# A scan's output tiles from a pool of four, and a convolution's kernels by one transfer

## The chip, the cores and the metric

The kernel runs on one core of one Trainium2 chip. The metric is the device time of one execution in microseconds (us), taken over several runs; a profile of one execution stands beside it. The engines are named as in the profile: PE is TensorE's matmul and PEld its weight load, DVE is VectorE, ACT is ScalarE, POOL is GpSimd, SP is SyncE, whose queue issues most transfers.

## The reference

One layer of a hybrid network runs over two sequences with the same weights: 256 context tokens and 2048 latent tokens of 1024 channels. What matters here, cut down:

```
h = rms_norm(x, g_pre) * (1 + scale) + shift
z, xbc, dt_raw, ga, gb, gsil = split(h @ w_in)
# group (i): a scan in chunks of 128 tokens, in both directions
xs, b_in, c_in = split(silu(depthwise_conv(xbc, width 5)))
y = scan_forward + scan_backward + d_skip * xs        # 16 heads of 64 channels
y_ssd = rms_norm(y * silu(z), norm_g)
# group (ii): gated depthwise convolution of width 31
hc = depthwise_conv(ga * sigmoid(gb), conf_conv_w) + conf_conv_b
y_conf = silu(layer_norm(hc)) * silu(gsil)
out = x + gate * rms_norm(concat(y_ssd, y_conf) @ w_out, g_post)
```

For the context the convolution of group (ii) runs along the 256 tokens. For the latent tokens, a grid of 32 rows by 64 columns, it runs down the rows, each column for itself. Besides the two outputs the final scan states of the context are returned.

## The kernel before

The 18 chunks of 128 tokens (two of context, sixteen of latent) are worked in two halves of ten and eight. In each half the input projection is computed channel block by channel block (128 channels), as three matmuls of split float32 operands for every 128 rows of the weights (mm_cm, L428 to L436). load_w (L384) fetches the weights. In the second half it reads the split weights that the first half has stored (wh and wl from whd and wld, L390 and L391, 512 KB each), into a pool of three buffers each.

The order of the projection blocks is: the xbc blocks, with their short convolution and a store to XB (L535); eight gate units for the conformer group (gab_unit, tiles gb and ga, whose result gl is stored at L598 into GL); eight units for z and eight for gsil (silu_unit, tile sp, stored at L611). All of these are generators. The work of the scan and of the convolutions is laid in between them step by step (interleave, merge), and a scheduler with a simulated timeline then decides the final order on each engine outside the parts that are kept in program order by hand.

pass_a (L702) is the forward scan of one chunk, in two groups g of eight heads. It loads xT and bc (L705, L707), and decay rows lb through ScalarE's queue (load_lb, L718; four buffers for each direction). GpSimd masks them (L730), ScalarE takes the exponentials (el at L727, the decays at L738), VectorE mixes the two directions (L742, L743). TensorE transposes x (px, L750), makes the diagonal part py (L774), the state's part po (L781) and the new states pst (L787 to L789). The output tile of a group, yg, lives through three VectorE steps and a store: skip (L808) takes a tile from a pool of two and writes d_skip * x into it (L810); close (L813) adds py (L815) and the state's part (L817), and the store at L818 sends it to YP on SP's queue. skip of a later group therefore waits until the store of the tile two groups before has landed.

The latent convolution takes one block of 128 channels at a time, j = 0 to 7 (lat_conv, L673). It is a set of small matmuls: the kernels of a block come as a table kd (128 partitions of 32 by 32 values), are turned by ScalarE into kt (L679), and 256 matmuls of 32 by 32 by 64 (cp, L690) multiply kt with x, the gated input read back from GL. VectorE empties the banks into cvv (L694), and four stores a block go to CV (L699). lat_load (L663) fetches kd and x in four quarters of 32 partitions, kd from the padded kernel array wconv (L670), x from GL (L671); both have two buffers, so block j + 1 is fetched while block j is worked on. PSUM tiles of the scan and of this convolution share a ring of five banks ("ss").

In the second half the pool lp (L1015) holds kd, x (tile cx), kt, cvv, the biases cbb and the context convolution's buffers cg; it is opened when the pools of the short convolution are closed. The scan's other tiles are in pool pa, which is open over both halves. The eight blocks of the latent convolution and the last four of the context convolution (ctx_conv, L640) are laid between the projection units of the second half, together with the scan of chunks 9 to 17 (L1020 to L1029). Behind them the backward scan and the output projection follow, in an order written by hand from L1335 on.

Of the kernel before, what the change touches and what calls it, by code (L numbers as in the profile page):

```python
# [8 lines left out]
F32 = mybir.dt.float32  # L9
# [8 lines left out]
P = 128  # L18
# [66 lines left out]
def backbone_kernel(ctx, tc, xa, xt_in, cols, rows, wconv, conf_b, gp_row, bg_row, state0, w_mod, w_dt, w_in, w_out,  # L85
# [3 lines left out]
    V, S, T, DMA = (InOrder(tc, e) for e in (nc.vector, nc.scalar, nc.tensor, nc.sync))  # L89
# [30 lines left out]
    def place(i):  # L120

        return (0, i) if i < HT[0] else (1, i - HT[0])
# [66 lines left out]
    pa = ph_a.enter_context(tc.tile_pool(name="pa", bufs=1))  # L189
# [473 lines left out]
    def lat_load(j, lp):  # L663
        kd = lp.tile([P, 32, 32], F32, tag="kd", name=f"kd{j}", bufs=2)
        x = lp.tile([P, 32, 64], F32, tag="cx", name=f"cx{j}", bufs=2)
        lat_in[j] = kd, x
        for a in range(4):
            rs = slice(a * 32, (a + 1) * 32)
            src = bass.AP(tensor=wconv.tensor, offset=(j * 4 + a) * 64 * 32, ap=[[32, 32], [1, 1024]])
            DMA.dma_start(kd[rs].rearrange("p r g -> p (r g)"), src)  # L670
            DMA.dma_start(x[rs], GL[j][:, 256:].rearrange("(g a) (r w) -> a r g w", a=4, w=64)[a])  # L671

    def lat_conv(j, lp, cbb, more):  # L673
        if j not in lat_in:
            lat_load(j, lp)
        kd, x = lat_in.pop(j)
        yield
        kt = lp.tile([P, 32, 32], F32, tag="kt", name=f"kt{j}", bufs=1)
        S.copy(kt[:, :, ::-1].rearrange("p g r -> p r g"), kd)  # L679
        if more(j + 1):  # L680
            lat_load(j + 1, lp)
        yield
        vt = lp.tile([P, 32, 64], F32, tag="cvv", name=f"cvv{j}", bufs=1)
        for h in range(2):
            ps = {a: bank("ss", f"cp{j}_{a}") for a in (2 * h, 2 * h + 1)}
            for q in range(8):
                for u in range(4):
                    for a in ps:
                        rs = slice(a * 32, (a + 1) * 32)
                        T.matmul(ps[a][u * 32:(u + 1) * 32, q * 64:(q + 1) * 64], kt[rs, u * 8 + q, :], x[rs, u * 8 + q, :],  # L690
                                 start=True, stop=True)
            yield
            for a in ps:
                V.scalar_tensor_tensor(vt[:, a::4, :], ps[a].rearrange("p (c w) -> p c w", w=64), 0.5,  # L694
                                       cbb[:, j, a::4].unsqueeze(2).to_broadcast([P, 8, 64]), MUL, ADD)
            yield
        for u in range(4):
            c0 = j * P + u * 32
            DMA.dma_start(CV[c0:c0 + 32, 256:].rearrange("c (r w) -> r c w", w=64), vt[u * 32:(u + 1) * 32])  # L699


    def pass_a(i):  # L702
        half, il = place(i)
# [102 lines left out]
        yg = {}  # L806

        def skip(g):  # L808
            yg[g] = pa.tile([P, 4, P], F32, tag="yg", name=f"yg{i}{g}", bufs=2)
            V.tensor_tensor(yg[g], xT[:, 4 * g:4 * g + 4, :],  # L810
                            cv[:, C_D + 4 * g:C_D + 4 * g + 4].unsqueeze(2).to_broadcast([P, 4, P]), MUL)

# [35 lines left out]
        decay(0, 1)  # L848
        mask(1, 0)
        skip(0)  # L850
        load_lb(1, 1)
        yield
        weigh(0, 1)
        mix(0, 1)
        decay(1, 0)
        mask(1, 1)
        skip(1)
        yield
        diag(0, 0)
# [155 lines left out]
    lp = ph_l.enter_context(tc.tile_pool(name="lp", bufs=1, side="right"))  # L1015
# [122 lines left out]
    def norms(i, yz, nq):  # L1138

        pm = bank("ss", f"pm{i}")  # L1140
        src = [(c, e, t[1]) for c, e, t in ((0, 4.0 * EPS, yz), (1, EPS, nq)) if t]
        for c, e, t in src:
            T.matmul(pm[:, c:c + 1], t, ones[:, 0:1], start=True, stop=True)
        rs = []
        for c, e, t in src:
            ms = p1.tile([P, 1], F32, tag=f"ms{c}", name=f"yms{i}{c}", bufs=2)
            V.tensor_scalar(ms, pm[:, c:c + 1], 1.0 / D, e, MUL, ADD)
            rs.append((c, rstd_of(p1, ms, f"yr{i}{c}")))
        return rs
# [31 lines left out]
    def conf_load(i):  # L1181
        n = p2.tile([P, 8, P], F32, tag="cn", name=f"cn{i}", bufs=2)
        DMA.dma_start(n, CV[:, i * P:(i + 1) * P].rearrange("(c p) t -> p c t", p=P))
        return n
# [20 lines left out]
    def gs_load(i):  # L1205
        gs = p2.tile([P, 8, P], F32, tag="gs", name=f"gsl{i}", bufs=1)
        DMA.dma_start(gs, chan_slice(GS, i))
        return gs
# [57 lines left out]
    i = order[0]  # L1266
# [21 lines left out]
    for b in range(2):  # L1288
        for m, u in enumerate(last):
            run(take(u, 8))  # L1290
            if b == 0 and m == 1:
                rs = norms(i, yz, None)
# [18 lines left out]
            if b == 1 and m == 0:  # L1311
                rs = norms(i, None, nq)
                nq = conf_sqsum(i1, vv[1][0])
            if b == 1 and m == 1:
                n, v = nn[0], vv[0][0]
# [3 lines left out]
            if b == 1 and m == 2:  # L1319
                gs0, v0, n = gs_load(i), v, nn[1]  # L1320
# [17 lines left out]
    i, nxt, nx2 = order[:3]  # L1338
    banks(i)
    out_part(pso[i], yh, 0, 1)  # L1340
    rs = norms(nxt, yz, nq)
# [42 lines left out]
    n, n2 = n2, conf_load(order[3])  # L1384
    yh = yhn

    for a, i in enumerate(order[1:], 1):
# [7 lines left out]
        rs = None if last else norms(nxt, yz, nq)  # L1395
# [46 lines left out]
        if a + 3 < NT:  # L1442
            ssd_load(order[a + 3])
            n, n2 = n2, conf_load(order[a + 3])
        else:
            n = n2
# [72 lines left out]
```

## Time and profile before

| | |
|---|---|
| time, median of 3 runs | 1862.05 us (1860.89 to 1865.44) |
| the profiled execution's own time | 1862.69 us |
| its span, first to last instruction | 1860.9 us |
| mean granted TensorE clock | 0.983 |
| PE busy | 1797.5 us |
| DVE, ACT, POOL busy | 1212.7, 867.4, 167.5 us |
| transfers on SP's queues and ACT's queue, all together | 375.22 MB, mean 202 GB/s |

The stretches: until about 270 us the first half's xbc blocks, from 270 to 730 us the first half's scan, until 917 us the second half's xbc blocks, from 917 to about 1330 us the second half's scan with the latent convolution, then the backward scan and the output projection. Times in the answers of the trace are counted from the span's start. A row of the timeline gives start, duration, engine, line, operation, tiles and shape, and in brackets the engine's idle time before it with what ended it; "SPq" and "ACTq" rows are the issue of transfers on these queues, and their duration is that of the issue, not of the transfer. In the chain that ended last, a DMA row is the time from issue to landing. The granted clock of a stretch is a share of TensorE's full speed.

### The profile page before, as it was taken

The numbers are of one execution on the slowest core, as the hardware profiler recorded it, in microseconds if no ns is written. First come the engines' busy times: TensorE is split into PE (matmuls) and PEld (weight loads), VectorE is DVE, ScalarE is ACT, GpSimd is POOL, SyncE is SP. The second block draws the span as 40 slices with busy tenths as digits, with TensorE's granted clock in tenths as the row PEclk, the third lists the DMA queues.
The fourth block names the chain that finished last, engine by engine and source line by source line (L and its number), as shares of the span: only waits on it lengthen the run. The fifth ranks groups of instructions, "written<-read, shape, count | busy, mean of one in ns | idle before, by whom it ended". The sixth has DMA issues, their size and how long they took to land.

```text
span 1860.9 us, 29891 instructions
## 1 busy us (share of the span) xinstructions
PE 1797.5 (97%) x11167; PEld 1482.9 (80%) x11167; DVE 1212.7 (65%) x1846; ACT 867.4 (47%) x1958; POOL 167.5 (9%) x281
## 2 busy tenths in 40 slices
PE   5899999999999999999999889899999999999998
PEld 3688887888888888888877667677887888888886
DVE  4488867565666762587457475868347887777763
ACT  4646424444465441834235445553245545454441
POOL 0002001111111000100001011110000111111110
PEclk9899999999999999999999899899999999999999
DMA  9556565574776664446598799685877666566632
GB/s 319 201 202 224 198 222 196 168 237 153 239 271 232 202 214 162 163 152 210 175 223 239 163 255 227 220 226 193 278 237 247 184 184 170 173 171 170 187 102 79
DMA packets 304253, 375.22 MB, mean 202 GB/s; under 512 B 84198, under 2 KB 203622, under 8 KB 304108
## 3 DMA queue, kind: packets, MB, share of 16 engines
q1 hardware_dynamic: 283372, 335.56, 58.1%
q10 hardware_dynamic: 20736, 37.76, 7.1%
q8 instruction: 88, 1.44, 0.3%
q14 instruction: 57, 0.47, 0.1%
HBM read 243.66 MB, written 129.59 MB: 201 GB/s over the span
## 4 chain that ended last, share of the span: by engine, by line
PE 84%; DMA 8%; ACT 2%; DVE 2%; issue 1%; SPq 1%; POOL 0%; ACTq 0%; POOLq 0%; DVEq 0%
PE op L81 20%; PE sp L433 7%; PE sp L434 7%; PE sp L435 7%; PE xp L434 5%; PE xp L435 5%; PE xp L433 5%; PE ga L433 3%; PE ga L435 2%; PE ga L434 2%; DMA lb<-lt 2%; PE gb L433 2%; PE gb L435 2%; PE gb L434 2%; PE py L774 2%; PE po L781 2%
## 5 line engine op out<-in xcount | busy, mean ns | idle before, releaser
L738 ACT ACTIVATE lb<-lb,WB 128x128 f32<-128x128 f32 x576 | 184.4, 391 | 173.5 <-POOL lb L730 159.6
L433 PE MATMUL sp<-hh,wh 128*128 128x512 f32 (+1 forms) x640 | 239.9, 375 | 0.0
L435 PE MATMUL sp<-hh,wl 128*128 128x512 f32 (+1 forms) x640 | 237.3, 371 | 0.0
L434 PE MATMUL sp<-hl,wh 128*128 128x512 f32 (+1 forms) x640 | 237.3, 371 | 0.0
L433 PE MATMUL xp<-hh,wh 128*128 128x512 f32 (+1 forms) x464 | 171.4, 371 | 2.0 <-ACT hh L329 2.0
L434 PE MATMUL xp<-hl,wh 128*128 128x512 f32 (+1 forms) x464 | 171.7, 370 | 0.0
L435 PE MATMUL xp<-hh,wl 128*128 128x512 f32 (+1 forms) x464 | 171.5, 370 | 0.0
L730 POOL TENSOR_SCALAR_AFFINE_SELECT lb<-lb 128x512 f32<-128x512 f32 x144 | 105.2, 733 | 730.4 <-ACT el L727 392.1
L530 DVE SCALAR_TENSOR_TENSOR cva<-raw,cwh,cva 128x1280 f32<-128x1280 f32 (+1 forms) x96 | 142.0, 1487 | 19.6 <-ACT cva L524 17.6
L435 PEld LDWEIGHTS sp<-hh,wl 128*128 128x128 f32 x640 | 121.4, 190 | 21.1
L433 PEld LDWEIGHTS sp<-hh,wh 128*128 128x128 f32 x640 | 121.7, 190 | 20.6
L434 PEld LDWEIGHTS sp<-hl,wh 128*128 128x128 f32 x640 | 121.6, 190 | 20.0
L433 PE MATMUL ga<-hh,wh 128*128 128x512 f32 (+1 forms) x320 | 121.1, 378 | 5.0 <-DMA wh<-whd 4.7
L75 DVE SCALAR_TENSOR_TENSOR cg<-cg,cv 128x256 f32<-128x256 f32 x240 | 121.2, 505 | 3.3
L433 PE MATMUL gb<-hh,wh 128*128 128x512 f32 (+1 forms) x320 | 120.4, 376 | 0.6 <-DVE gth L597 0.6
L435 PE MATMUL ga<-hh,wl 128*128 128x512 f32 (+1 forms) x320 | 119.1, 372 | 0.0
L434 PE MATMUL ga<-hl,wh 128*128 128x512 f32 (+1 forms) x320 | 118.8, 371 | 0.0
L435 PE MATMUL gb<-hh,wl 128*128 128x512 f32 (+1 forms) x320 | 118.5, 370 | 0.0
L434 PE MATMUL gb<-hl,wh 128*128 128x512 f32 (+1 forms) x320 | 118.4, 370 | 0.0
L742 DVE TENSOR_TENSOR lb<-lb,lb 128x512 f32<-128x512 f32 x72 | 50.5, 702 | 92.0 <-ACT lb L738 70.6
L433 PEld LDWEIGHTS xp<-hh,wh 128*128 128x128 f32 x464 | 88.1, 190 | 16.9 <-ACT hh L329 2.3
L434 PEld LDWEIGHTS xp<-hl,wh 128*128 128x128 f32 x464 | 87.9, 189 | 14.3
(269 smaller groups left out, 3758.6 us busy)
## 6 DMA issues: line engine op xcount, KB each, us to landing
lb<-lt ACTq DMA_DIRECT2D x144, 256.0 KB, 4.4
wr<-in_w_in SPq DMA_DIRECT2D x88, 256.0 KB, 5.4
whd<-wh SPq DMA_DIRECT2D x44, 512.0 KB, 4.0
wld<-wl SPq DMA_DIRECT2D x44, 512.0 KB, 5.2
wh<-whd SPq DMA_DIRECT2D x44, 512.0 KB, 4.3
wl<-wld SPq DMA_DIRECT2D x44, 512.0 KB, 5.9
xT<-xb SPq DMA_DIRECT2D x18, 512.0 KB, 4.1
yp<-yg SPq DMA_DIRECT2D x36, 256.0 KB, 4.6
```

The lines of the kernel that those rows point to most:

```text
L75: return self._tc.keep_in_program_order(getattr(self._eng, name)(*a, **k))
L81: return lambda *a, **k: self._tc.keep_in_program_order(f(*a, **k))
L433: T.matmul(ps[:, :BN], wh[:, k, :], hh[:, k, :], start=(k == 0), stop=False)
L434: T.matmul(ps[:, :BN], wh[:, k, :], hl[:, k, :], start=False, stop=False)
L435: T.matmul(ps[:, :BN], wl[:, k, :], hh[:, k, :], start=False, stop=(k == KT - 1))
L530: V.scalar_tensor_tensor(a[:, :n], raw[:, t:t + n], cwh[:, ct * 5 + t:ct * 5 + t + 1], a[:, :n], MUL, ADD)
L730: G.affine_select(E[g, hq, d], E[g, hq, d], pattern=[[0, 4], [sg, P]], compare_op=ALU.is_ge, fill=NEG, base=0, channel_multiplier=-sg)
L738: S.activation(lb[:, h, :], lb[:, h, :], AF.Exp, bias=WB[:, i, c + h:c + h + 1])
L742: V.tensor_tensor(a, a, E[g, hq, 1], ADD)
L774: T.matmul(py[g][j * HD:(j + 1) * HD, q * P:(q + 1) * P], xt[g][:, h * HD:(h + 1) * HD], E[g, hq, 0][:, t, :], start=True, stop=True)
L781: T.matmul(po[g][:, q * P:(q + 1) * P], Sf[g][:, q * P:(q + 1) * P], bc[:, 2 + g, :], start=True, stop=True)
```

## The change

Two places are edited. In lat_load the four transfers of kd, one for each quarter of 32 partitions, become one transfer of 512 KB, placed ahead of the four transfers of x. Its source is written as four blocks (2048 values apart) of 32 rows (32 values apart) of 1024 values; the bytes and their places are the same. In skip, the tile yg of a chunk of the second half comes from pool lp with four buffers; in the first half it comes from pa with two, as before. No arithmetic is changed.

```diff
     def lat_load(j, lp):
         kd = lp.tile([P, 32, 32], F32, tag="kd", name=f"kd{j}", bufs=2)
         x = lp.tile([P, 32, 64], F32, tag="cx", name=f"cx{j}", bufs=2)
         lat_in[j] = kd, x
+        src = bass.AP(tensor=wconv.tensor, offset=j * 4 * 64 * 32, ap=[[64 * 32, 4], [32, 32], [1, 1024]])
+        DMA.dma_start(kd.rearrange("p r g -> p (r g)"), src)
         for a in range(4):
             rs = slice(a * 32, (a + 1) * 32)
-            src = bass.AP(tensor=wconv.tensor, offset=(j * 4 + a) * 64 * 32, ap=[[32, 32], [1, 1024]])
-            DMA.dma_start(kd[rs].rearrange("p r g -> p (r g)"), src)
             DMA.dma_start(x[rs], GL[j][:, 256:].rearrange("(g a) (r w) -> a r g w", a=4, w=64)[a])
...
         def skip(g):
-            yg[g] = pa.tile([P, 4, P], F32, tag="yg", name=f"yg{i}{g}", bufs=2)
+            pool, n = (lp, 4) if half else (pa, 2)
+            yg[g] = pool.tile([P, 4, P], F32, tag="yg", name=f"yg{i}{g}", bufs=n)
             V.tensor_tensor(yg[g], xT[:, 4 * g:4 * g + 4, :],
```

## The prediction

> **What bounds the kernel now.** I read the page's busy times first, then the busy times by stretch for the part in which the edited code runs, then the waits of TensorE there.
>
> ```profile
> PE 1797.5 (97%) x11167; PEld 1482.9 (80%) x11167; DVE 1212.7 (65%) x1846; ACT 867.4 (47%) x1958; POOL 167.5 (9%) x281
> ```
>
> ```profile
> 270.00:730.00 460.00, 459.07 (x2604) 382.24 (x2603) 291.39 (x503) 213.04 (x526) 48.15 (x76) 1.00 0.62 211
> 917.00:1330.00 413.00, 387.24 (x3866) 307.83 (x3865) 256.87 (x443) 179.69 (x438) 42.97 (x64) 0.95 0.82 217
> ```
>
> TensorE is the bound, with 97% of the span. The second fence compares the first half's scan (270 to 730 us) with the second half's scan and latent convolution (917 to 1330 us); columns are length, busy time of PE, PEld, DVE, ACT and POOL, then clock, DMA share and GB/s. In the first TensorE is idle for 460.00 - 459.07 = 0.9 us at full clock; in the second for 413.00 - 387.24 = 25.8 us, at a granted clock of 0.95. No matmul of the change is added or taken away, so a gain can only come out of those 25.8 us and the slow matmuls around them. These are the waits behind them (engine, line, waited for: total us, times, longest):
>
> ```profile
> PE pst L787 <- DVE cvv L694: 5.1, 1, 5.1
> PE ga L433 <- DMA wh<-whd: 4.7, 1, 4.7
> PE cp L690 <- DVE yg L815: 4.6, 1, 4.6
> PE px L750 <- issue: 3.0, 1, 3.0
> PE pst L787 <- ACT xwh L764: 2.0, 1, 2.0
> PE cp L690 <- issue: 2.0, 1, 2.0
> PE po L781 <- DVE yg L815: 2.0, 1, 2.0
> ```
>
> Seven stalls make 23.4 of the 25.8 us. The change acts on a different list, the waits of VectorE for a free yg tile. For line 810 in this stretch the trace answers:
>
> ```profile
> DVE yg L810: 17.7, 6
> ```
>
> Six waits, 17.7 us of VectorE, not of TensorE. What matters is which of them stands under one of the seven.
>
> **The pool of four, first place (1007 to 1018 us).** The timeline, with start, duration, engine, line and the idle time before in brackets:
>
> ```profile
> 1005.88 0.69 DVE L742 TENSOR_TENSOR lb<-lb,lb 128x512 f32<-128x512 f32 x1 [1.83 <-issue]
> ...
> 1008.09 0.31 PE L690 MATMUL cp<-cx,kt 32*32 32x64 f32 x6
> ...
> 1011.01 0.69 DVE L810 TENSOR_TENSOR yg<-xT,cv 128x512 f32<-128x512 f32 x1 [4.44 <-DMA yp<-yg]
> ...
> 1012.22 0.68 DVE L815 TENSOR_TENSOR yg<-yg,py 128x512 f32<-128x512 f32 x1
> ...
> 1012.96 2.03 PE L690 MATMUL cp<-cx,kt 32*32 32x64 f32 x122 [4.56 <-DVE yg L815]
> ...
> 1016.36 0.63 PE L433 MATMUL gb<-hh,wh 128*128 128x512 f32 x1
> 1016.79 0.63 PE L434 MATMUL gb<-hl,wh 128*128 128x512 f32 x1
> ...
> 1018.32 0.47 PE L433 MATMUL ga<-hh,wh 128*128 128x512 f32 x1
> ```
>
> VectorE stands at L810 until an older yp store has landed; L815, which empties the py bank that the convolution needs, starts 1.21 us after L810, with one instruction between. With four buffers L810 starts when L742 ends, at 1006.57; L815 follows at 1007.8 and ends near 1008.5, when TensorE has just done the six matmuls that it could do. About 0.15 us of 4.56 stays: 4.4 us gained. The matmuls after the stall start 0.43 us apart (1016.36, 1016.79); the undisturbed distance stands below, 0.23. From 1012.96 to 1018.32 TensorE runs at about that half speed: 5.3 us x (1 - 0.23/0.43) = 2.5 us. Without the stall this goes too. Sum here: **6.9 us**.
>
> **The pool of four, second place (1048 to 1062 us).**
>
> ```profile
> 1048.46 6.21 SPq L671 DMA_DIRECT2D cx<-gl  x4
> ...
> 1054.76 1.27 SPq L818 DMA_DIRECT2D yp<-yg  x1
> ...
> 1055.82 2.45 ACT L738 ACTIVATE lb<-lb,WB 128x128 f32<-128x128 f32 x8 [2.95 <-POOL lb L730]
> ...
> 1060.34 0.69 DVE L810 TENSOR_TENSOR yg<-xT,cv 128x512 f32<-128x512 f32 x1 [8.95 <-DMA yp<-yg]
> 1060.95 0.68 DVE L742 TENSOR_TENSOR lb<-lb,lb 128x512 f32<-128x512 f32 x1
> 1061.55 1.28 DVE L694 SCALAR_TENSOR_TENSOR cvv<-cp,cbb 128x512 f32<-128x512 f32 x2
> ...
> 1062.03 2.02 ACT L679 COPY kt<-kd 128x1024 f32<-128x1024 f32 x1 [3.76 <-DVE lb L742]
> ...
> 1062.29 0.79 PE L787 MATMUL pst<-xwh,bth 128*128 128x512 f32 x1 [5.13 <-DVE cvv L694]
> ```
>
> The yp store is queued behind four cx loads that hold SP's queue for 6.21 us, so the buffer comes free late and VectorE loses 8.95 us. TensorE waits for the first of the two L694, which empties a bank. Without the wait L810 runs at 1051.4, but the next thing is late too: L742 needs the eight decays of ScalarE, which end at 1055.82 + 2.45 = 1058.3. Then L694 starts at 1058.9 and TensorE at 1059.6 instead of 1062.29. **2.6 us** of 5.13 are gained; the other 2.5 stay, and with them the slow matmuls. That a gap so short slows the clock is seen at the po matmuls, 13 us earlier:
>
> ```profile
> 1049.03 2.07 PE L781 MATMUL po<-bc,Sf 128*128 128x128 f32 x8 [1.98 <-DVE yg L815]
> ...
> 1051.33 0.63 PE L788 MATMUL pst<-xwl,bth 128*128 128x512 f32 x1
> 1051.76 0.63 PE L789 MATMUL pst<-xwh,btl 128*128 128x512 f32 x1
> ```
>
> After 1.98 us of idle the distance is again 0.43 us. The Trainium skill, "TensorE: Matmul & The Clock Gate", Part 1, has it that only an idle window of about 3.4 us takes the clock down; by that rule the 2.5 us left would leave the clock alone and the sum would be higher by an estimated 2.5 us, the ramp of the first place. The trace disagrees, and I go by the trace.
>
> The other stalls of TensorE keep their causes: the 3.0, 2.0 and 2.0 us waits and that at po have no yg wait of VectorE under them. The new tiles add no wait: they lie where the buffers of the phase before lay, and the first of them is written at 969.5, 52 us into the stage:
>
> ```profile
> L810 DVE TENSOR_TENSOR yg<-xT,cv x16: 675/684/1119, 969.5 to 1285.8; 128x512 f32<-128x512 f32 x16
> ```
>
> **One transfer in place of four.** It removes 24 of 32 issues on SP:
>
> ```profile
> L670 SPq DMA_DIRECT2D kd<-in_wconv x32: 311/420/1633, 920.7 to 1167.7; - x32
> ```
>
> At the median of 420 ns this is 24 x 0.42 = 10 us of SP's queue, worth something only where TensorE waits for a transfer behind it. There is one such place:
>
> ```profile
> 1070.65 2.52 SPq L670 DMA_DIRECT2D kd<-in_wconv  x3
> ```
>
> and in the chain that ended last:
>
> ```profile
> 1067.98 0.23 PE ga L435
> ...
> 1073.27 7.45 DMA wh<-whd
> ...
> 1080.86 0.77 PE ga L433
> ...
> 1086.68 0.24 PE ga L433
> ```
>
> Three kd issues (2.52 us) stand ahead of the weights that TensorE awaits for 4.7 us. After 1080.86 it is slow for 5.8 us, which costs 5.8 x 0.465 = 2.7, so this stall is worth 7.4 us in all. Bounds: at best the weights leave 2.5 us sooner and the stall shrinks to 2.2; at worst the 512 KB now go out together ahead of other loads of the same queue and one or more further stalls of 7.4 us arise. What is queued behind the new instruction while it waits for the kernel copy L679 is what was queued behind the first quarter before: convolution stores, scan loads, weights. I take **0**, since the same bytes still share the queue with those weights, and both the copy (3.0 us sooner, with VectorE) and TensorE (2.6) shift alike.
>
> **Sum.** 6.9 + 2.6 + 0 = 9.5 us, against the profiled execution's own 1862.69 us (span 1860.9 and 1.8 around it): 1853.2. It was 0.6 us above the median 1862.05, so the forecast is 1852.5 us. Below, 0.3% (5.6 us) is what a measurement of this kernel can tell from no change.
>
> **The rivals.** (a) *Another chain takes the place.* The scheduler writes the order of every engine anew, and the scan's decay loads are late by themselves: in the second place they already keep half the stall, and the po stall is theirs. If the first place keeps 4 us and its slow clock as well, 9.5 shrinks to about 3 and the time is 1859. For it: the 0.82 DMA share. Against it: at 1006.57 nothing but L810 is seen to hold VectorE, which goes through the next two without a gap. Chance 0.16.
>
> (b) *The merged transfer is slow and makes weights late.* Its source is four blocks of 32 rows, its destination 128 partitions. If the hardware spreads it by the outer count, four engines of the sixteen move it, each 128 KB instead of 32.
>
> ```profile
> q1 hardware_dynamic: 283372, 335.56, 58.1%
> ...
> kd<-in_wconv SPq DMA_DIRECT2D x32, 128.0 KB, 6.5
> ```
>
> The queue's 335.56 MB took 58.1% of 16 engines x 1860.9 us, 19.4 GB/s for an engine that is busy, so 128 KB are 6.8 us on each of the four, against 1.7 spread out. Whatever SP issues next would then wait about 5 us on these four, with the copy of weights among it. Each late copy is priced as the one above, 7.4 us. One gives 1852.5 + 7.4 = 1859.9, no measurable change; two, 1867.3, still just inside; from the third on the kernel is slower: 1874.7. For it: one copy is late already, and SP more than once waits for the weights' buffer to come free before it can issue at all:
>
> ```profile
> SPq L390 <- PE ga L435: 12.8, 2, 9.2
> ```
>
> Against it: no transfer of the trace has such a shape, and kd itself is loaded a block ahead. The Trainium skill, "DMA: Bandwidth & Descriptors", "Why a DMA increments its semaphore by 16 and not by 1", says that a transfer takes the largest number of engines up to 16 that divides the slowest dimension of both sides; by that it would be four. No run here shows it. Chances: 0.13 for one or two late copies, 0.21 for more.
>
> (c) *The edit does nothing where it counts*: were the yg waits only a cover for later ones, both places would keep their stalls and the time stay at 1862; that is in (a).
>
> **How the numbers follow.** The forecast's case has 0.50. Its own range runs from all three stalls gone with their slow clock (6.9 + 6.9 + 7.4 = 21.2 us, 1841) to the first place alone (6.9, 1855.2). Case (a) and the mild (b) lie between 1856.5 and 1867.6: 0.16 + 0.13 = 0.29. The harsh (b) is slower: 0.21. The range reaches from 1840 to 1871: above it the half of the harsh (b) with three full stalls or more is left out, below it a few per cent for an order that happens to be better throughout.
>
> **What would show it.** Right: no idle time at L810 put down to the yp store; no 4.6 us at the convolution's matmuls after L815; TensorE busy above 395 of the 413 us of this stage; a granted clock above 0.95 there; the weights' wait near 4.7 us. Wrong, towards (a): L810 free, but the same seconds lost to lb or el. Wrong, towards (b): kd landing well above the 6.5 us of a quarter, and waits of TensorE or its weight loads for wh and wl. A stall outside the stage that differs by more than a microsecond would show that the order changed elsewhere, which this sum leaves out.

## The result and the profile after

The changed kernel takes 1889.21 us (median of 4 runs, 1885.13 to 1892.6) against 1861.47 us for the kernel before on the same chip: a ratio of 1.0143, 95% interval 1.0124 to 1.0162. The medians lie 27.7 us apart; the ratio, taken over all the runs, makes it 26.6. The prediction said 1852.5 us, a little faster, and allowed 1871 at most. The profiled execution took 1890.1 us, its span is 1888.4 us.

The stage to look at runs from the first gb matmul of the second half to the first matmul of the backward scan (qo). The stretches view gives it for the kernel before (length, busy time of PE, PEld, DVE, ACT, POOL, then clock, DMA share, GB/s):

```profile
902.97:1357.50 454.53, 428.77 (x4054) 342.29 (x4052) 276.99 (x462) 196.56 (x458) 43.21 (x68) 0.96 0.82 226
```

and for the changed kernel, with the 413 us that the prediction looked at ahead of it:

```profile
917.00:1330.00 413.00, 364.61 (x3624) 287.56 (x3623) 252.93 (x433) 176.25 (x433) 44.10 (x68) 0.95 0.77 205
905.67:1385.60 479.93, 431.54 (x4056) 342.40 (x4055) 282.22 (x464) 197.47 (x459) 44.10 (x68) 0.95 0.78 216
```

The stage is 25.4 us longer for the same matmuls. TensorE's idle time in it rises from 25.8 to 48.4 us, its busy time by 2.8 us. The DMA share falls from 0.82 to 0.78: the stage waits for transfers while the engines that carry them have, on average, more room than before. The other 2 us of the difference of spans lie ahead of the stage, where the edited code does not run and the profiled executions differ by several microseconds (the stage starts between 901.0 and 909.7 us in the profiles shown here). The first half's scan (270 to 730 us) stays full, with TensorE busy for 456.76 of 460 us.

TensorE's waits in the stage, changed kernel (total us, times, longest):

```profile
PE cp L690 <- DMA cx<-gl: 12.1, 2, 11.2
PE ga L433 <- DMA wh<-whd: 6.9, 1, 6.9
PE po L781 <- DVE yo L795: 6.8, 1, 6.8
PE px L750 <- issue: 4.2, 1, 4.2
PE sp L433 <- DVE sth L610: 3.7, 1, 3.7
PE cp L690 <- DVE cvv L694: 3.6, 1, 3.6
...
PE cp L690 <- DVE yg L816: 0.9, 1, 0.9
```

The first of the stalls that the pool was to remove (4.6 us at cp, behind yg) is down to 0.9, and the wait of 5.1 at pst is gone from the list. But cp now waits 11.2 us for the input cx of the first latent block. The chain of waits of the changed kernel shows what led there (start, duration, what):

```profile
931.68 0.26 SPq L391
...
932.03 15.79 DMA gl<-gth
...
947.84 0.33 SPq L671
...
948.21 10.49 DMA cx<-gl
...
958.75 2.03 PE cp L690 x118
```

and SP's part of its timeline, what was in the queue then:

```profile
923.52 0.67 SPq L668 DMA_DIRECT2D kd<-in_wconv  x1
...
925.29 0.58 SPq L668 DMA_DIRECT2D kd<-in_wconv  x1
...
932.03 0.38 SPq L598 DMA_DIRECT2D gl<-gth  x1
...
947.84 8.66 SPq L671 DMA_DIRECT2D cx<-gl  x4
```

Two merged kernel transfers, 1.8 us apart, go out at 923.5 us. A store of gl issued 6.7 us behind the second needs 15.79 us to land; the list of transfers gives 5.0 us as the median for these stores. The loads of cx read what that store writes, so they can only be issued at 947.84, and the one that the chain goes through takes 10.49 us; a third kernel transfer had gone out at 940.02. The kernel before has, in its timeline and its list of waits:

```profile
920.73 1.84 SPq L670 DMA_DIRECT2D kd<-in_wconv  x4
...
929.50 0.32 SPq L598 DMA_DIRECT2D gl<-gth  x1
...
937.50 4.45 SPq L671 DMA_DIRECT2D cx<-gl  x4
...
PE cp L690 <- DMA cx<-gl: 0.3, 1, 0.3
```

There the same store was ready for the cx loads 8.0 us after its issue at the latest, and cp waited 0.3 us. The two later new stalls are of the same kind by their chains: the 6.8 us at po ends a chain through an xT load that takes 12.83 us (issued at 1185.34, right behind a kd transfer at 1183.68), the 3.6 us at cp one through convolution stores issued behind a kd transfer at 1047.41. Between that xT load and po stands skip (L811), where VectorE waits 4.23 us for xT, so the second part of the change has a hand in this stall too; more on that below.

### The profile page after: what moved, and what is told of

Same layout as the page of the kernel before. It is cut to its first block, busy times and chain, and to the rows that moved or that the text cites. A ratio compares the mean times of both kernels' runs of the same rounds, so it can differ in the third digit from the quotient of the medians.

```text
span 1888.4 us, 29863 instructions
## 1 busy us (share of the span) xinstructions
PE 1800.1 (95%) x11167; PEld 1482.4 (79%) x11167; DVE 1215.2 (64%) x1846; ACT 867.0 (46%) x1958; POOL 169.4 (9%) x281
## 3 DMA queue, kind: packets, MB, share of 16 engines
q1 hardware_dynamic: 282892, 335.55, 57.3%
## 4 chain that ended last, share of the span: by engine, by line
PE 74%; DMA 12%; DVE 5%; ACT 3%; issue 3%; POOL 1%; SPq 1%; ACTq 0%; POOLq 0%; DVEq 0%
PE op L81 20%; PE sp L433 6%; PE sp L434 5%; PE sp L435 5%; DMA lb<-lt 4%; PE xp L434 4%; PE xp L435 4%; PE xp L433 4%; PE ga L433 2%; PE ga L435 2%; PE gb L433 2%; PE ga L434 2%; PE gb L434 2%; PE gb L435 2%; ACT lb L738 1%
## 5 line engine op out<-in xcount | busy, mean ns | idle before, releaser
L727 ACT ACTIVATE el<-lb 64x256 f32<-64x256 f32 x136 | 56.3, 414 | 105.1 <-DMA lb<-lt 55.7
L610 DVE SCALAR_TENSOR_TENSOR sth<-sth,sp 128x512 f32<-128x512 f32 (+1 forms) x80 | 50.4, 630 | 80.4 <-ACT sth L609 75.5
```

The lines of the kernel that those rows point to most:

```text
L610: V.scalar_tensor_tensor(th, th, 1.0, ps[:, :BN], ADD, MUL)
L727: S.activation(el[g][rs, q:q + 2, :], E[g, hq, 0][rs, j::2, :], AF.Exp)
```

## The experiments

All times are medians in us; each ratio is to runs of the kernel before on the same chip, with its 95% interval.

| kernel | time | ratio |
|---|---|---|
| the change | 1889.21 | 1.0143 (1.0124 to 1.0162) |
| e1_pool: pool of four alone | 1862.52 | 0.9991 (0.9973 to 1.0009) |
| e2_kd: one transfer alone | 1892.4 | 1.0150 (1.0126 to 1.0174) |
| e3_spread: change, source of 128 rows | 1854.42 | 0.9953 (0.9940 to 0.9967) |
| e4_four_slow: before, sources of four blocks | 1882.69 | 1.0093 (1.0067 to 1.0119) |
| e7_outer8: change, eight blocks | 1867.9 | 1.0038 (1.0020 to 1.0056) |
| e7_outer4: change, four blocks | 1890.7 | 1.0153 (1.0116 to 1.0189) |
| e7_outer2: change, two blocks | 1915.79 | 1.0289 (1.0259 to 1.0319) |
| e5_spread_only: e3 without the pool | 1854.74 | 0.9955 (0.9937 to 0.9974) |
| e8_pool_held: e1 with skip held | 1853.16 | 0.9941 (0.9920 to 0.9961) |
| e9_spread_held: e3 with skip held | 1842.73 | 0.9886 (0.9866 to 0.9906) |
| e10_hold_only: before with skip held | 1857.87 | 0.9977 (0.9961 to 0.9993) |
| e11_change_held: change with skip held | 1877.37 | 1.0080 (1.0065 to 1.0096) |

### Each part alone

e1_pool is the kernel before with only the second hunk of the change, e2_kd with only the first.

> The pool of four alone, kd still by four transfers. Theory F (the merged transfer is moved by four of the sixteen engines, and what is queued behind it comes late): the loss is not here, so about 1852 us as the sum of the prediction had it, in any case under 1862; no gl store lands after more than 10 us at the stage's start, and no wait of over 10 us of TensorE for cx. Rival O (the pool of four lets the scheduler put L810 earlier in VectorE's order, where it then waits for xT and holds up what is behind it): about 1880 or more, as after the change. Rival T (one transfer of 512 KB is bad whatever its spread): same as theory F here.

> The merged transfer alone, yg from the pool of two. Theory F and rival T: slower than before, 1880 to 1900 us, with the first kernel copy again waiting until about 938 us and the gl store behind it landing after about 15 us. Rival O: about 1862 or a little under it, since SP issues 24 instructions less.

The one transfer alone costs 1.0150, the whole loss, and by the same path: in its profile the store of gl takes 13.41 us and TensorE's longest wait for cx is 8.5 us. The pool of four alone gives nothing that can be measured (0.9991), and the 1852 us expected of it did not come. So the loss lies in the transfer, and there is a second question: why the pool gave none of the forecast 9.5 us.

### The transfer: its size, or the shape of its source

e3_spread keeps one transfer of 512 KB, but the host lays the kernel windows out as 128 separate rows for each block, so that the source is one list of 128 rows. No work is left out; wconv only holds the windows one by one, where they overlapped before.

```diff
-        src = bass.AP(tensor=wconv.tensor, offset=j * 4 * 64 * 32, ap=[[64 * 32, 4], [32, 32], [1, 1024]])
+        src = bass.AP(tensor=wconv.tensor, offset=j * 128 * 1024, ap=[[1024, 128], [1, 1024]])
```

e4_four_slow is the other way round: the kernel before with its four transfers, the source of each written as four blocks of eight rows (the blocks stand apart in the host's layout, so they stay blocks).

```diff
-             src = bass.AP(tensor=wconv.tensor, offset=(j * 4 + a) * 64 * 32, ap=[[32, 32], [1, 1024]])
+             src = bass.AP(tensor=wconv.tensor, offset=(j * 4 + a) * 36 * 1024, ap=[[9 * 1024, 4], [1024, 8], [1, 1024]])
```

> The change as it is, but the kernel windows are laid out by the host as 128 rows of 1024 values per block (copies, no arithmetic), so the source's outer count is 128 instead of 4; one transfer of the same 512 KB. The order of the instructions is that of the changed kernel. Theory F: kd lands in 4 to 7 us instead of about 14 us, the gl store behind it within 6 us, and the time falls by the whole loss, to 1850 to 1860 us. Rival T: unchanged near 1889 us. Rival O: unchanged near 1889 us.

> The kernel before, with the four quarter transfers kept, but each quarter's source written as four blocks of eight rows with a gap between them (the host's layout is padded; same bytes moved). Pool of two, TensorE's order as before. Theory F: each quarter is moved by four engines too, so the time rises as after the change, 1875 to 1900 us, with kd quarters landing well above 6.5 us. Rival T and rival O: as before, 1862 us within 5 us.

One transfer with a flat source makes the kernel faster than before (0.9953); four transfers with sources of four blocks make it slower (1.0093). It isn't the merging that costs, it is the four blocks. Why the four transfers lose 17 us and the one transfer 28 stays open. In e3_spread TensorE's waits in the stage hold no wait for cx at all, and the weights' wait is that of before:

```profile
PE ga L433 <- DMA wh<-whd: 4.7, 1, 4.7
PE px L750 <- issue: 3.9, 2, 2.4
PE cp L690 <- issue: 3.4, 1, 3.4
PE px L750 <- ACT sb L803: 2.9, 1, 2.9
```

The list of transfers of e3_spread gives the landing of the single one (KB, median us from issue to landing):

```profile
kd<-in_wconv SPq DMA_DIRECT2D x8, 512.0 KB, 6.7
```

512 KB in 6.7 us, about what one quarter of 128 KB took before (6.5). The list pairs only two of the eight landings here, and none for the changed kernel. The trace's record of semaphore updates has them all: the last update of a kd transfer comes 4.3 to 7.6 us after the issue in e3_spread, and 9.3 to 19.0 us after it in the changed kernel.

### The dose

If the outer count of the source sets how many DMA engines carry the transfer, the cost must fall with it step by step. Three versions of the changed kernel, the same bytes in the same rows of 4 KB, differ only in how the rows are grouped: two blocks of 64, four of 32, eight of 16, one unused row between blocks. For eight:

```diff
-        src = bass.AP(tensor=wconv.tensor, offset=j * 4 * 64 * 32, ap=[[64 * 32, 4], [32, 32], [1, 1024]])
+        src = bass.AP(tensor=wconv.tensor, offset=j * 136 * 1024, ap=[[17 * 1024, 8], [1024, 16], [1, 1024]])
```

> The same with two blocks of 64 rows: outer count two. Theory F: two engines with 256 KB each, kd lands in over 25 us, and everything of the SP queue behind it waits that long on these two; far slower, 1920 us or more. Rival L: as the spread version.

> The changed kernel with the windows laid out by the host as four blocks of 32 rows with an unused row behind each block, so the source keeps an outer count of four. It is the control for the spread experiment, which had a new layout too. Theory F (the outer count sets the number of engines): as after the change, 1880 to 1895 us. Rival L (the overlapping rows of the old layout were the slow thing, not the outer count): as the spread version, 1850 to 1860 us.

> The same with eight blocks of 16 rows: outer count eight, same bytes, same order of all instructions. Theory F: eight engines with 64 KB each, kd lands in about 8 to 10 us, time between the spread version and the changed kernel, 1855 to 1870 us. Rival L: as the spread version.

Two, four and eight blocks and (e3_spread) 128 rows in the outer dimension give 1.0289, 1.0153, 1.0038 and 0.9953. The version with four blocks equals the change (1.0143), so neither the gap nor the other layout costs anything that shows. The place where it hurts follows as well. TensorE's wait for cx in e7_outer2:

```profile
PE cp L690 <- DMA cx<-gl: 22.9, 2, 21.8
PE ga L433 <- DMA wh<-whd: 12.3, 2, 10.6
PE po L781 <- DVE yo L795: 10.4, 2, 9.3
```

in e7_outer8:

```profile
PE ga L433 <- DMA wh<-whd: 5.9, 1, 5.9
PE px L750 <- issue: 5.7, 2, 4.2
PE cp L690 <- DMA cx<-gl: 4.7, 2, 3.4
```

The longest wait for cx is 21.8, 11.2 (the change), 3.4 us and none. The expected times held but for that of two blocks: 1920 us or more, against 1915.79 measured. The Trainium skill, "DMA: Bandwidth & Descriptors", "Why a DMA increments its semaphore by 16 and not by 1", has a transfer use the largest number of engines up to 16 that divides the slowest dimension of both sides; that would be two, four, eight and sixteen here, and the four times stand in that order. A count on the profile's page bears out the numbers themselves. The queue's lines (packets, MB, share of 16 engines) of two, four and eight blocks and of 128 rows are:

```profile
q1 hardware_dynamic: 282876, 335.55, 55.9%
q1 hardware_dynamic: 282892, 335.55, 57.0%
q1 hardware_dynamic: 282924, 335.55, 58.3%
q1 hardware_dynamic: 282988, 335.55, 57.7%
```

The kernel before has 283372 packets, so these have 496, 480, 448 and 384 fewer, and the pages' counts of packets under 512 B fall by the same numbers: the data packets are the same, only small ones are gone. If each engine that takes part in a transfer adds one small packet to it, the 32 transfers before add 32 x 16 = 512, and eight transfers on two, four, eight and sixteen engines add 16, 32, 64 and 128, which gives these four differences exactly. The change has 282892 as well; e4_four_slow, with 32 transfers, has 282988, which is four engines for each. That a small packet stands for an engine is read from this fit.

### The pool: why it gave nothing

e5_spread_only asks whether the pool gives something once the transfer is flat: it is e3_spread with the second hunk of the change undone, so yg has its pool of two again.

> The spread single transfer alone, yg from the pool of two as before. If the two parts add up, the spread version's gain of 0.5% minus the pool's 0.1% is left for the merge alone: about 1855 us. If the pool's gain only shows once SP's queue is lighter, this one is near 1860.

0.9955 against 0.9953: again nothing. VectorE's waits at skip show an exchange, first in e5_spread_only, then in e3_spread:

```profile
DVE yg L810 <- DMA yp<-yg: 21.9, 7, 8.8
...
DVE yg L811 <- DMA xT<-xb: 14.2, 5, 5.7
```

With two tiles it waits for stores of yp, with four for loads of xT. The profile of e1_pool shows the same in single steps. The forecast stalls did go, or shrink: in its timeline TensorE now waits 1.38 us at the first place and 3.42 at the second. But there is a new wait of VectorE 200 us later.

```profile
1017.59 0.66 PE L750 MATMUL px<-ident,xT 128*128 128x128 f32 x4 [1.38 <-ACT sb L803]
...
1059.73 0.57 PE L787 MATMUL pst<-xwh,bth 128*128 128x512 f32 x1 [3.42 <-DVE cvv L694]
...
1255.74 1.29 DVE L811 TENSOR_TENSOR yg<-xT,cv 128x512 f32<-128x512 f32 x2 [7.72 <-DMA xT<-xb]
```

TensorE's waits of e1_pool from 917 to 1330 us:

```profile
PE px L750 <- issue: 5.8, 2, 4.3
PE ga L433 <- ACT el L727: 4.1, 1, 4.1
PE pst L787 <- DVE cvv L694: 3.4, 1, 3.4
PE sp L433 <- DVE sth L610: 2.3, 1, 2.3
```

With tiles free early, the scheduler puts skip of the next chunk (both groups, "x2") far ahead in VectorE's order. There it waits 7.72 us for xT, which has a single buffer and is still on its way, and everything behind it on VectorE waits too: sth for 2.3 us of TensorE's time, then px for 4.3 (the profile names no releaser there; with skip held, below, neither stall is left). In the kernel before, this skip ran some 17 us later and waited for nothing:

```profile
1273.04 0.69 DVE L810 TENSOR_TENSOR yg<-xT,cv 128x512 f32<-128x512 f32 x1
```

The wait for the store was gone, and a wait for a load had taken its place. "Nothing" is to be read within the noise: in e1_pool's profile the stage is 5.3 us shorter than before (449.2 against 454.5), but it starts 5.4 us later, and by the ratio of all the runs 1.7 us are left.

To test that, skip's instruction in the second half is held behind a second mixing instruction (L743) of its own chunk: that of heads 0 to 3 for the first group, that of heads 4 to 7 for the second. TensorE's order of instructions is left as it was by this.

```diff
-            V.tensor_tensor(a, a, cb[:, g, :].unsqueeze(1).to_broadcast([P, 4, P]), MUL)
+            mixed[g, hq] = V.tensor_tensor(a, a, cb[:, g, :].unsqueeze(1).to_broadcast([P, 4, P]), MUL)
...
+            if half:
+                with tc.issue_after(mixed[0, g].ins):
+                    V.tensor_tensor(yg[g], xT[:, 4 * g:4 * g + 4, :],
```

> The kernel before with the pool of four alone, and skip's VectorE instruction of the second half held behind the second mix instruction of its own chunk. The pool alone (without the hold) took 0.9991 of the time before: the stalls at 1007 to 1017 us went, and new ones of 2.25 and 4.28 us stood at 1257 to 1274 us, where line 811 waited 7.72 us for xT. Theory (with four buffers the instruction moves ahead on VectorE into the next chunk's xT load, and that wait eats the gain): held back, line 811 waits for no load in the second half, the stalls near 1257 and 1274 us are absent, and the time is 1852 to 1857 us, a ratio of 0.995 to 0.998. Rival (the pool's waits were only cover for others, as the decay loads): another stall stands in their place and the ratio stays within 0.998 to 1.001, about 1861 us.

> The change with the windows laid out as 128 rows of 1024 for each block (one transfer over all engines), the pool of four, and skip's VectorE instruction held as in the other kernel of this call. Without the hold it took 0.9953 of the time before, the same as without the pool of four (0.9955). Theory (the moved instruction eats the pool's gain): 0.990 to 0.993, 1843 to 1849 us, with no wait for xT at line 811 in the second half. Rival (the pool has nothing to give once other waits stand there): 0.994 to 0.997, about 1853 us.

Both came out on the theory's side, at 0.9941 and 0.9886, each with its ratio a little below the range that the theory gave. The hold lets the scheduler move some other VectorE instructions as well, so the price of the wait for xT by itself is not isolated. In e8_pool_held the source line of skip's held instruction (here L813) has sixteen instructions and nothing that its engine waited for:

```profile
L813 DVE TENSOR_TENSOR yg<-xT,cv x16: 676/683/1124, 984.3 to 1276.6; 128x512 f32<-128x512 f32 x16
its engine sat idle before it (us, times) until:
who waited for it (us, times):
```

Two controls separate the hold from the pool and from the transfer.

> The kernel before, with its pool of two and its four transfers, and skip's VectorE instruction of the second half held behind the second mix instruction of its own chunk. Pool and hold together took 0.9941 of the time before, the pool alone 0.9991. Theory (the pool takes the store's wait away and the hold takes the load's wait away; neither does it alone): the wait for the yp store at line 810 stays, the TensorE stalls of about 4.6 and 5 us at 1007 to 1062 us stay, and the ratio is 0.998 to 1.002, 1859 to 1866 us. Rival (a better order of VectorE's work was all that was gained, and the pool of four is not needed for it): 0.993 to 0.996, about 1852 us.

> The changed kernel (its transfer on a source of four blocks) with skip's instruction held as in the other kernel of this call. Theory (the two costs are separate: the transfer's lateness stays whole, the hold brings what it brought elsewhere, 0.005 to 0.007): 1.0143 becomes 1.007 to 1.010, 1875 to 1881 us. Rival (the late loads set the time of the stage whatever VectorE's order): 1.012 to 1.016, about 1888 us.

e10_hold_only, 0.9977, lies between the two expectations: the hold alone brings something, which the theory denied, and the waits that were to stay mostly went. Its skip line shows how:

```profile
L812 DVE TENSOR_TENSOR yg<-xT,cv x16: 676/683/1123, 980.1 to 1280.2; 128x512 f32<-128x512 f32 x16
...
  DMA yp<-yg: 1.9, 1
```

Issued later, skip finds the old tile's store landed and waits 1.9 us in place of 17.7. So part of the gain is a better place for the instruction, with two buffers or with four. The pool adds the rest: 0.9977 to 0.9941, 0.0036 or 6.7 us, with an interval of about 0.0010 to 0.0062 from those of the two ratios. e11_change_held, 1.0080, is as expected: the hold brings 0.0063 there, 0.0050 with the pool alone and 0.0067 with the flat transfer. Within the noise the costs of the two parts are separate.

e9_spread_held is the best kernel of the study, 1842.73 us against 1862.47 for the kernel before on the same chip. Its stretch and its waits:

```profile
917.00:1330.00 413.00, 402.18 (x3967) 320.44 (x3966) 272.49 (x456) 190.44 (x449) 47.06 (x68) 0.98 0.87 238
```

```profile
PE px L750 <- ACT sb L803: 3.0, 1, 3.0
PE ga L433 <- DMA wh<-whd: 2.8, 1, 2.8
PE px L750 <- DVE cvv L694: 1.6, 1, 1.6
```

TensorE is idle for 10.8 of 413 us, where the kernel before had 25.8.

## Why the prediction was wrong

**One transfer in place of four: this step failed.** The prediction had "I take **0**, since the same bytes still share the queue with those weights". The bytes are the same, but not the time for which they hold those DMA engines that carry them: the packet counts give four engines for each transfer, and it landed after 9.3 to 19.0 us. Against the pool alone the measured term is 1.0143 - 0.9991 = 0.0152, 28 us. Rival (b) named the mechanism, with 0.34 for both its forms, and three things in it were off. It looked for the damage at the weights, because the one late load in the profile before was theirs: their wait rose by 2.2 us only (4.7 to 6.9). It hit the shortest loop through memory, gl stored and read back as cx, and then xT and the convolution's stores. Its price of a late copy, 7.4 us, was a stall of the kernel before; here the first stall alone is 11.2 us, since store and load follow each other and both are late. And "kd itself is loaded a block ahead" spoke for kd, not for what stands behind it in the queue. The range stopped at 1871 us, short even of its own three stalls (1874.7), and the time came out 18 us above it.

**The other bound of the same step was too narrow as well.** Fewer issues were to bring 2.5 us at best. With the transfer spread, they bring 0.0045 (8 us) alone, 0.9991 - 0.9953 = 0.0038 (7 us) with the pool and 0.9941 - 0.9886 = 0.0055 (10 us) with the hold too. In e3_spread the weights' wait is still 4.7 us, so the gain came at other places than the one copy that the chain showed; which ones stays open. That e3_spread's source rows also lie elsewhere in memory isn't separated from this; at four blocks the layout made no difference.

**The pool, first and second place: right where they looked.** In e1_pool the stall of 4.56 us is gone; of the 5.13 us 3.42 stay, where 2.5 were forecast. **"The new tiles add no wait" failed.** No wait for the memory shows, but the order changed: a free tile let the instruction move ahead into a wait for xT. Of 9.5 us the pool alone gave 0.9 parts in a thousand, 1.7 us (between -1.7 and 5.0). That is rival (a) in kind, though not with the decay loads it named, and it had kept 3 us. Held in place, pool and hold give 11 us, 6.7 of them the pool's. That this is near the forecast's 9.5 us is chance, since the forecast knew nothing of the hold.

**Of the signs to look for**, TensorE's busy time told the truth and the clock did not. TensorE "above 395 of the 413 us" held in neither the change (364.61) nor e1_pool (389.66), and did in e8_pool_held (396.34) and e9_spread_held (402.18). The granted clock was 0.98 in e1_pool, above the 0.95 asked for, with a time that had not changed. For kd's landing the list of transfers had no value, so the sign of rival (b) had to be read from the store behind it and from the semaphores.

## What to carry to other kernels

Before merging transfers, look at the outermost dimension of both sides: if the merged one has a small count there, lay the data out so that it is large, or leave the transfers apart. Price a slow transfer by what stands behind it in its queue, and first by data that are stored and read back, where two transfers are late in a row. When a tile gets more buffers, ask which wait held its first writer in place by chance, and where in its engine's order it goes without it.

## What the runs showed of the hardware

A transfer slowed others of the same queue that had nothing to do with it: a 256 KB store behind two transfers of four blocks took 15.79 us, where the same store before took 8.0 at most. The cost was steep: from 128 rows to two blocks, eight transfers of 512 KB, 4 MB of the 335.55 MB that the queue moves, made the kernel 3.4% slower (0.9953 to 1.0289). One transfer of 512 KB with 128 rows landed in 6.7 us, one of 128 KB with 32 rows in 6.5. One with four blocks needed 9.3 to 19.0 us, and by the packet counts four of the sixteen engines carried it.
